# One pool for two attentions, shared places, and q and k split at their projection, in a hybrid decoder layer on one Trainium2 core

## The chip, the cores and the metric

The kernel runs on one core of one Trainium2 chip. The metric is the time of one execution on the device in microseconds (us). Five engines work side by side and meet through semaphores: PE (TensorE, matmuls; PEld is its weight load), DVE (VectorE), ACT (ScalarE), POOL (GpSimd) and SP (SyncE, which only issues transfers here). ACT and POOL issue transfers too. Each engine executes its own instructions in a fixed order.

## The reference, cut to what matters

```python
h = rms_norm(x, norm_mix_g)
proj = h @ w_in                                  # (1024, 1024) @ (1024, 5896)
# dilated attention: 3 groups (window, step) = (128,1), (512,4), (2048,16), 4 heads of 64 each
o_g, lse_g = dilated_window_attention(q_g, k_g, v_g, window, step, slopes)
o_a = sum(softmax(lse over groups) * o_g)        # (1024, 256)
# forgetting attention ("fox"), 8 heads of 64, causal, decay = cumsum(log_sigmoid(f))
o_b = softmax(q k^T / 8 + c_t - c_s) @ v         # (1024, 512)
gates = sigmoid(proj[gate columns] + b_gate)     # (1024, 2048)
x = x + (g_a * (o_a @ w_dil_out) + g_b * (o_b @ w_fox_out)) @ w_out
x = x + (silu(h2 @ w_g) * (h2 @ w_u)) @ w_ffn_down     # h2 = rms_norm(x), width 2816
return rms_norm(x, norm_final_g)
```

Everything is fp32; sequence 1024, width 1024.

## The kernel before, in words

Operands of the large products are kept as two fp32r halves, hi and lo (`split`, L94: ACT writes hi, DVE writes lo = source - hi), and a product is three matmuls, hi·hi, hi·lo and lo·hi (`mm3`, L98). Tiles live in pools; a pool that is opened takes the places of one that was closed, and a tile's first write waits until what stood in its place has been read for the last time. The code is written in one order, and a scheduler then lays down the order of each engine, so that a matmul of a later line can stand between two of an earlier one.

The stages, in the order of time: the norm and the value projections; the sums of the normed input for a seven-product scheme; six calls of `projections` (L279), four for the q and k of fox, two for four q and k tiles of the dilated attention; fox (`fox_qk`, `fox_scores`, `fox_values`); the dilated attention (`dil_qk`, `dil_scores`, `dil_values`); the merge with the gates; the output product; the feed-forward part.

**A call of projections** (L279) makes two 128-column blocks. It loads two raw weight tiles (`raw_w`, tag "wr", two places), and `left_side` (L252) makes four operands of them: A1 (split of the first raw tile), S12 and S34 (sums on POOL, L264, L265, L268, L269, then split) and A22 (split of half the second raw tile, two places). Seven groups of twelve matmuls (`prod`, L272) follow. In the order on PE a call overlaps the next: S12 of call n+1 stands ahead of A22 of call n. At the end the two result tiles "qo" are joined on DVE and stored by POOL (L314).

**Fox** takes four pairs of heads. For each, `fox_qk` loads q and k in eight transfers of 64 rows through SP (L558), ACT casts (L559) and DVE takes the remainders (L563, L566). `fox_scores` makes the scores of 512 queries (b = 0 or 1) of one head with two matmuls per key block (L583, L584), ACT adds the decay (L587), POOL masks (L590), DVE takes the maxima and POOL reduces them over partitions (L598). `fox_values` subtracts and sums on DVE (L611, L614, L623), exponentiates on ACT (L617) and multiplies with the values (L634) and with ones (L637); `finish` (L323) divides. Values of one unit are written behind the scores of the next one.

**The dilated attention** does the like in four units (u, b): scores L342, evicted on DVE (L700, L710, L720), maxima and sums in `over_keys` (L734), POOL's reduction L726, subtraction L747 to L755, exponentials on ACT, values L780 and ones L783. Its pools "dil" and "dila" open after fox's "fox" and "foxa" have been closed; its q and k come by `dil_qk` (L677, ACT's queue), its values by `load_vd` (L665, POOL's queue).

**Fill.** `ahead` (L214) is a plain projection of one block, 48 matmuls with 512 columns (L99 to L101, tile "pf"): 8 blocks of q and k of the dilated attention (`BESIDE`) and 16 blocks of gates. The scheduler puts these 1152 matmuls between those of the attentions, where PE would wait. ACT evicts each half (L224) into one tile "fst" of 4 KB per partition and stores it with one transfer (L225). The last gate may only start behind the last values of the dilated attention (L807).

Behind the attentions the pool "gates" opens; its first tile "oh" lies on the places of "fst". `load_o` (L819) brings the attentions' results and splits them, and the merge's matmuls (L189, L190, L193) begin.

Of the kernel before, what the change touches and what calls it, by code (L numbers as in the profile page):

```python
# [8 lines left out]
F32 = mybir.dt.float32  # L9
F32R = mybir.dt.float32r  # L10
# [5 lines left out]
P = 128  # L16
# [31 lines left out]
def layer_kernel(  # L48
# [34 lines left out]
    o_dram = dpool.tile([6, P, S], F32, name="o_dram")  # L83

# [119 lines left out]
    fqk_dram = dpool.tile([2, 4, P, S], F32, name="fqk_dram")  # L204
# [9 lines left out]
    def ahead(pool, c0, dst, dl=1, sc=1.0):  # L214

        pf = [psf.tile([P, HALF], F32, tag="f", name=nm("pf")) for _ in range(2)]
        w = load_w(w_in[:, c0:c0 + P], KT, P)
        for hh in range(2):
            for k in range(KT):
                mm3(pf[hh][:], w[:, k], hT[hh][:, k], k == 0, k == KT - 1)  # L220
        n = HALF // dl
        st = pool.tile([P, dl, S // dl], F32, tag="fst", name=nm("fst"), bufs=2)
        for hh in range(2):
            nc.scalar.activation(out=st[:, :, hh * n:(hh + 1) * n], in_=view(pf[hh][:], dl), func=AF.Copy, scale=sc)  # L224
        nc.scalar.dma_start(out=dst, in_=st[:].rearrange("p r i -> p (r i)"))  # L225
# [26 lines left out]
    def left_side(pool, rg, ru, bufs):  # L252
# [9 lines left out]
        S34, A22, A1 = pair(KT, "s34", 1), pair(4, "a22", 2), pair_of(rg[:])  # L262
# [16 lines left out]
    def projections(pool, T, c, dst, dls, sc):  # L279
# [33 lines left out]
        for o, d in zip((o2, o1), dst[::-1]):  # L313
            nc.gpsimd.dma_start(out=d, in_=o[:].rearrange("p r i -> p (r i)"))  # L314
# [93 lines left out]
    with pool_of("comb1", 1) as tpool:  # L408
# [90 lines left out]
        with pool_of("proj", 1) as upool:  # L499
            cums = [upool.tile([P] + d, F32, name=n, bufs=1) for n, d in (  # L500
                ("sums", [2, P]), ("az", [NT * 8]), ("u", [NT * 8]), ("t1", [NT * 8]), ("tot", [NT, 8]))]
            for pr in range(0, 4, 2):
                for a in range(2):
                    c0 = FOX0 + a * FOX_W + pr * P
                    projections(upool, T, (c0, c0 + P), [fqk_dram[a, pr + i] for i in range(2)], (1, 1), 1.0)
# [40 lines left out]
    with pool_of("fox", 1) as spool:  # L546
        vf = spool.tile([P, NT, 4, 2, DH], F32, name="vf", bufs=1)
        nc.gpsimd.dma_start(out=vf[:].rearrange("p t a b d -> p t (a b d)"), in_=vf_dram.rearrange("t p c -> p t c"))

        def fox_qk(pool, ql, pr):  # L550
# [3 lines left out]
            for a, xs, sc in ((0, qx, SCALE), (1, kx, 1.0)):  # L554
                for e in range(2):
                    raw = pool.tile([P, S], F32, tag="qraw", name=nm("qraw"), bufs=2)
                    for at in half:
                        nc.sync.dma_start(out=raw[at, :], in_=fqk_dram[a, pr, half[e], :])  # L558
                    nc.scalar.activation(out=xs[e][:], in_=raw[:], func=AF.Copy, scale=sc)  # L559
                    rows = half[e] if a == 0 else half[1 - e]  # L560
                    hi = xs[e][rows, :].bitcast(F32)
                    if a == 0:
                        nc.vector.scalar_tensor_tensor(out=ql[e][rows, :], in0=raw[rows, :], scalar=sc, in1=hi,  # L563
                                                       op0=ALU.mult, op1=ALU.subtract)
                    else:
                        nc.vector.tensor_tensor(out=xs[e][rows, :], in0=raw[rows, :], in1=hi, op=ALU.subtract)  # L566
# [75 lines left out]
        with pool_of("foxa", 2) as apool:  # L642
            pend = None
            ql = [apool.tile([P, S], F32R, name=f"ql{e}", bufs=1) for e in range(2)]
            for e in range(2):
                nc.gpsimd.memset(ql[e][half[1 - e], :].bitcast(F32), 0.0)
            for pr in range(4):
                qk = fox_qk(apool, ql, pr)
                for b in range(2):
                    unit = [fox_scores(apool, qk, 2 * pr + e, b) for e in range(2)], pr, b  # L650
                    if pend:
                        fox_values(apool, *pend)
                    pend = unit
            fox_values(apool, *pend)

    for u, g, a in BESIDE:
        ahead(fpool, dil_cols(u, g, a), dqk_dram[u, g, a], STR[a][g], (SCALE, 1.0)[a])


    with pool_of("dil", 1) as spool:  # L660
        vd, last_pv = [None, None, None], [None]

        def load_vd(pool, g):
            vd[g] = pool.tile([P, NT, 2, 2, DH], F32, tag=f"vd{g}", name=nm("vd"), bufs=1)
            nc.gpsimd.dma_start(out=vd[g][:].rearrange("p t a b d -> p t (a b d)"),  # L665
                                in_=vd_dram[g].rearrange("t p c -> p t c"))

        load_vd(spool, 0)
        load_vd(spool, 1)

        def dil_qk(pool, u):

            qk = [[None, None] for _ in range(3)]
            for g in range(3):
                for a in range(2):
                    qk[g][a] = pool.tile([P, STR[a][g], S // STR[a][g]], F32, tag=f"qk{g}{a}", name=nm("dqk"), bufs=1)
# [3 lines left out]
        def dil_scores(pool, qk, u, b):  # L680
# [3 lines left out]
            L0, L2, Mx, L1 = [[pool.tile([P] + d, F32, tag=n, name=nm(n), bufs=bufs) for e in range(2)]  # L684
                              for n, d, bufs in (("L0", [NT, P], 3), ("L2", [4, P], 3),
                                                 ("Mx", [HALF], 4), ("L1", [2, 2, 256], 3))]
# [72 lines left out]
        def dil_values(pool, scs, u, b, o):  # L759
# [24 lines left out]
            finish(pool, po, den, o[:, b::2])  # L784
            if b == 1:
                nc.gpsimd.dma_start(out=o_dram[u], in_=o[:])

        with pool_of("dila", 1) as apool:
            pend = None
            for u in range(2):  # L790
                qk = dil_qk(apool, u)
                for b in range(2):
                    scs = dil_scores(apool, qk, u, b)
                    if b == 0:
# [291 lines left out]
```

## Time and profile before

| what | value |
|---|---|
| median of 3 runs | 1523.96 us (1522.74 to 1524.77) |
| the profiled execution's own time | 1522.51 us |
| its span, first to last instruction | 1520.2 us |
| granted TensorE clock, mean | 0.992 |
| first fox score (L583) on PE | 290.16 us from the start |
| first dilated score (L342) | about 521 us |
| last dilated values and ones (L780, L783) | end at about 651.7 us |
| first matmul of the merge (L189) | 668.21 us |

A row of the page or of a list of groups has line, engine, operation, output<-inputs, shapes and count; behind the first bar the busy time in us and the mean of one in ns, behind the second bar the idle time of the engine just before, and what ended it. A row of the timeline begins with start and duration in us; in brackets stands the idle time before it and who ended it. A row of the windows has the stretch, its length, then for each engine the busy time and the number of instructions, the granted TensorE clock, the share of the transfer engines and GB/s.

### The profile page before, as it was taken

The numbers are of one execution on the slowest core, as the hardware profiler recorded it, in microseconds if no ns is written. First come the engines' busy times: TensorE is split into PE (matmuls) and PEld (weight loads), VectorE is DVE, ScalarE is ACT, GpSimd is POOL, SyncE is SP. The second block draws the span as 40 slices with busy tenths as digits, with TensorE's granted clock in tenths as the row PEclk, the third lists the DMA queues.
The fourth block names the chain that finished last, engine by engine and source line by source line (L and its number), as shares of the span: only waits on it lengthen the run. The fifth ranks groups of instructions, "written<-read, shape, count | busy, mean of one in ns | idle before, by whom it ended". The sixth has DMA issues, their size and how long they took to land.

```text
span 1520.2 us, 18124 instructions
## 1 busy us (share of the span) xinstructions
PE 1472.8 (97%) x6956; PEld 1192.0 (78%) x6956; DVE 894.1 (59%) x1321; ACT 536.8 (35%) x808; POOL 418.4 (28%) x351
## 2 busy tenths in 40 slices
PE   7999999999999999789999999999999999999997
PEld 6899888867777777568888788888888877888886
DVE  6482433398898399936628854444444445856546
ACT  5232221476566132335315432222222225312113
POOL 1012321273353011100000155555555553140000
PEclk9999999999999999989999999999999999999999
DMA  8132334733332732155613122222222225642202
GB/s 257 42 98 63 111 97 121 226 113 102 110 99 69 257 122 66 56 181 180 242 56 139 42 69 84 83 83 83 84 83 83 84 97 197 204 139 84 96 15 97
DMA packets 139045, 171.60 MB, mean 113 GB/s; under 512 B 6992, under 2 KB 108368, under 8 KB 138960
## 3 DMA queue, kind: packets, MB, share of 16 engines
q1 hardware_dynamic: 118096, 105.95, 23.5%
q0 software_dynamic: 9616, 34.62, 6.1%
q10 hardware_dynamic: 11248, 29.89, 5.3%
q8 instruction: 54, 0.88, 0.2%
q14 instruction: 31, 0.25, 0.1%
HBM read 123.25 MB, written 47.19 MB: 112 GB/s over the span
## 4 chain that ended last, share of the span: by engine, by line
PE 85%; DMA 4%; DVE 3%; ACT 3%; POOL 3%; issue 2%; SPq 0%; ACTq 0%; POOLq 0%; DVEq 0%
PE pd L276 26%; PE pd L99 10%; PE pd L100 10%; PE pd L101 10%; PE pf L100 5%; PE pf L101 5%; PE pf L99 5%; DMA wr<-in_w_ffn_in_dram 2%; PE pd L189 2%; PE pd L634 2%; PE pd L190 2%; PE pd L193 2%; ACT wh L95 2%; POOL sg L994 1%; PE pd L780 1%
## 5 line engine op out<-in xcount | busy, mean ns | idle before, releaser
L96 DVE TENSOR_TENSOR wl<-wr,wh 128x1024 fp32r<-128x1024 f32 (+2 forms) x152 | 165.9, 1095 | 147.3 <-ACT wh L95 146.7
L95 ACT ACTIVATE wh<-wr 128x1024 fp32r<-128x1024 f32 (+2 forms) x152 | 140.6, 932 | 316.2 <-PE pd L100 91.9
L276 PE MATMUL pd<-hT_t,wh 128*128 128x512 f32 x784 | 242.2, 390 | 1.4 <-ACT cc L289 0.7
L276 PE MATMUL pd<-tT,wh 128*128 128x512 f32 x672 | 206.9, 389 | 0.4 <-DVE v L909 0.4
L276 PEld LDWEIGHTS pd<-hT_t,wh 128*128 128x128 f32 x784 | 147.0, 188 | 32.4 <-ACT c L977 1.1
L276 PE MATMUL pd<-hT_t,wl 128*128 128x512 f32 x392 | 153.9, 393 | 1.7 <-DVE wl L96 1.5
L99 PE MATMUL pf<-hT_t,wh 128*128 128x512 f32 x384 | 151.0, 393 | 0.6 <-ACT fst L224 0.6
L100 PE MATMUL pf<-hT_t,wh 128*128 128x512 f32 x384 | 151.0, 393 | 0.0
L101 PE MATMUL pf<-hT_t,wl 128*128 128x512 f32 x384 | 150.9, 394 | 0.0
L276 PEld LDWEIGHTS pd<-tT,wh 128*128 128x128 f32 x672 | 126.1, 188 | 27.0 <-DVE v L909 0.8
L99 PE MATMUL pd<-wh,wh 128*128 128x512 f32 x352 | 137.6, 392 | 3.4 <-DVE acc L1037 1.9
L100 PE MATMUL pd<-wl,wh 128*128 128x512 f32 x352 | 137.1, 389 | 0.0
L101 PE MATMUL pd<-wh,wl 128*128 128x512 f32 x352 | 137.0, 389 | 0.0
L276 PE MATMUL pd<-tT,wl 128*128 128x512 f32 x336 | 130.1, 390 | 0.0
L1037 DVE TENSOR_TENSOR acc<-pd,acc 128x512 f32<-128x512 f32 x128 | 85.6, 685 | 69.2 <-PE pd L101 69.1
L264 POOL TENSOR_TENSOR s<-wr 128x512 f32<-128x512 f32 x26 | 38.9, 1496 | 312.8 <-DVE tT L96 196.0
L96 DVE TENSOR_TENSOR wl<-s,wh 128x1024 fp32r<-128x1024 f32 x52 | 64.7, 1246 | 66.6 <-ACT wh L95 63.7
L95 ACT ACTIVATE wh<-s 128x1024 fp32r<-128x1024 f32 x52 | 55.1, 1060 | 126.5 <-POOL s L265 95.1
L276 PEld LDWEIGHTS pd<-hT_t,wl 128*128 128x128 f32 x392 | 73.6, 188 | 22.2 <-DVE wl L96 7.3
L101 PEld LDWEIGHTS pf<-hT_t,wl 128*128 128x128 f32 x384 | 72.1, 188 | 19.8 <-issue 5.0
L99 PEld LDWEIGHTS pf<-hT_t,wh 128*128 128x128 f32 x384 | 72.1, 188 | 19.7 <-issue 4.6
L100 PEld LDWEIGHTS pf<-hT_t,wh 128*128 128x128 f32 x384 | 72.1, 188 | 18.5 <-issue 4.1
(228 smaller groups left out, 2776.8 us busy)
## 6 DMA issues: line engine op xcount, KB each, us to landing
wr<-in_w_in_dram SPq DMA_DIRECT2D x46, 512.0 KB, 4.3
wr<-in_w_ffn_in_dram SPq DMA_DIRECT2D x44, 512.0 KB, 4.3
wr<-a_dram SPq DMA_DIRECT2D x22, 512.0 KB, 4.3
wr<-in_w_ffn_down_dram SPq DMA_DIRECT2D x22, 512.0 KB, 3.7
a_dram<-a POOLq DMA_DIRECT2D x20, 512.0 KB, 5.0
qraw<-fqk_dram SPq DMA_DIRECT2D x32, 256.0 KB, 4.2
g_dram<-fst ACTq DMA_DIRECT2D x16, 512.0 KB, 2.9
land<-g_dram SPq DMA_DIRECT2D x16, 512.0 KB, 3.4
```

Source lines behind the costliest of these rows:

```text
L95: nc.scalar.activation(out=hi, in_=src, func=AF.Copy)
L96: return nc.vector.tensor_tensor(out=lo, in0=src, in1=hi.bitcast(F32), op=ALU.subtract)
L99: nc.tensor.matmul(psum, w.hi, m.hi, start=start, stop=False)
L100: nc.tensor.matmul(psum, w.hi, m.lo, start=False, stop=False)
L101: last_mm[0] = nc.tensor.matmul(psum, w.lo, m.hi, start=False, stop=stop)
L189: nc.tensor.matmul(pt[hh][:], w.hi[:, k], m.hi, start=(k == 0), stop=False)
L190: nc.tensor.matmul(pt[hh][:], w.hi[:, k], m.lo, start=False, stop=False)
L193: nc.tensor.matmul(pt[hh][:], w.lo[:, k], m.hi, start=False, stop=(k == kt - 1))
L264: nc.gpsimd.tensor_tensor(out=s12[:, :4], in0=u1, in1=u2, op=ALU.add)
L276: last_mm[0] = nc.tensor.matmul(bank[:], p, q, start=first and k == 0 and n == 0, stop=k == 3 and n == 2, skip_group_check=True)
L634: nc.tensor.matmul(po[half[e], HALF - width[j]:], vf[:, j, pr, e], L[:, off[j]:off[j + 1]], start=(j == nj - 1), stop=(j == 0), skip_group ...
L1037: nc.vector.tensor_tensor(out=acc[:, t, cs], in0=pt[:], in1=acc[:, t, cs], op=ALU.add)
```

## The change

- One pool "attention" holds the tiles of both attentions. Those of the second that take over places of the first carry the same tag: its q and k those of fox's kx, qx and ql, its values the place of vf, its L0 tiles those of fox's score tiles of b = 0; the places of fox's score tiles of b = 1 (`over`) hold its third value tile and half of its L0 and L1.
- The last `fox_values` is written behind the first `dil_scores`, so that scores of the second attention stand among the last values of the first.
- `projections` of fox's q and k splits its results (ACT into "qh", one place, DVE in place) and stores hi and lo; POOL issues four transfers per call in place of two. The scale is applied there. `fox_qk` only loads, ten transfers of 64 rows per pair, on ACT's queue; ACT's casts and DVE's remainders there go.
- A22 has one place in `projections` (it had two).
- `ahead` evicts and stores each half by itself, into tiles of half the size; for blocks with a step the store has pieces of 512/step elements.
- The dilated result is kept by halves of the queries and put in order when it is split for the merge.

```diff
-    fqk_dram = dpool.tile([2, 4, P, S], F32, name="fqk_dram")
+    fqk_dram = dpool.tile([2, 4, 2, P, S], F32, name="fqk_dram")
...
-        st = pool.tile([P, dl, S // dl], F32, tag="fst", name=nm("fst"), bufs=2)
         for hh in range(2):
-            nc.scalar.activation(out=st[:, :, hh * n:(hh + 1) * n], in_=view(pf[hh][:], dl), func=AF.Copy, scale=sc)
-        nc.scalar.dma_start(out=dst, in_=st[:].rearrange("p r i -> p (r i)"))
+            st = pool.tile([P, dl, n], F32, tag="fst", name=nm("fst"), bufs=2)
+            nc.scalar.activation(out=st[:], in_=view(pf[hh][:], dl), func=AF.Copy, scale=sc)
+            nc.scalar.dma_start(out=dst.rearrange("p (r i) -> p r i", r=dl)[:, :, hh * n:(hh + 1) * n], in_=st[:])
...
-        S34, A22, A1 = pair(KT, "s34", 1), pair(4, "a22", 2), pair_of(rg[:])
+        S34, A22, A1 = pair(KT, "s34", 1), pair(4, "a22", bufs), pair_of(rg[:])
...
         for o, d in zip((o2, o1), dst[::-1]):
-            nc.gpsimd.dma_start(out=d, in_=o[:].rearrange("p r i -> p (r i)"))
+            flat = o[:].rearrange("p r i -> p (r i)")
+            if hl:
+                hi = pool.tile([P, S], F32R, tag="qh", name=nm("qh"), bufs=1)
+                split(hi[:], flat, flat)
+                nc.gpsimd.dma_start(out=d[0], in_=hi[:].bitcast(F32))
+                nc.gpsimd.dma_start(out=d[1], in_=flat)
...
+            for e in range(2):
+                q, k = [fqk_dram[a, pr, :, half[e], :] for a in range(2)]
+                for to, src in ((kx, k), (qx, (q[0], q[0]))):
+                    for i in range(2):
+                        nc.scalar.dma_start(out=to[e][half[i], :].bitcast(F32), in_=src[i])
+                nc.scalar.dma_start(out=ql[e][:DH, :].bitcast(F32), in_=q[1])
...
-            fox_values(apool, *pend)
...
+        for u in range(2):
+            qk = dil_qk(apool, u)
+            for b in range(2):
+                scs = dil_scores(apool, qk, u, b)
+                if u == b == 0:
+                    fox_values(apool, *pend)
+                    pend = None
+                    vd01 = apool.tile([P, 2, NT, 2, 2, DH], F32, tag="v", name="vd01", bufs=1)
+                    ov1, ov2 = over(), over()
...
+                if pend:
+                    dil_values(apool, *pend)
+                pend = scs, u, b
+        dil_values(apool, *pend)
```

How the order moves. In the rows below, numbers behind an L are lines of the file in question; the changed file's `split` is L96 and L97.

First, ACT in the middle of the projections, before: wh<-wr with 512 columns is A22, wh<-s is S34 and then S12, cc and qo evict PE's first bank.

```order
L289 ACTIVATE cc_1467<-pd_1496 128x512
L95 ACTIVATE wh_1474<-s_200_1489 128x1024
L289 ACTIVATE qo_1465<-pd_1496 128x512
L95 ACTIVATE wh_1732<-wr_1724 128x1024
L95 ACTIVATE wh_1739<-s_237_1736 128x1024
L95 ACTIVATE wh_1730<-wr_1726 128x512
L289 ACTIVATE cc_1594<-pd_1623 128x512
```

The same stretch in the changed kernel:

```order
L291 ACTIVATE cc_1483<-pd_1512 128x512
L96 ACTIVATE wh_1490<-s_204_1505 128x1024
L96 ACTIVATE qh_1451<-qo_1321 128x1024
L96 ACTIVATE wh_1636<-s_223_1633 128x1024
L291 ACTIVATE qo_1481<-pd_1512 128x512
L96 ACTIVATE wh_1764<-wr_1756 128x1024
L96 ACTIVATE wh_1627<-wr_1623 128x512
L96 ACTIVATE qh_1606<-qo_1482 128x1024
L291 ACTIVATE cc_1618<-pd_1647 128x512
```

Two splits of results (qh) have come in per call. The A22 that stands here is that of the next call in the changed kernel, where it was that of the call after the next; the load of the raw tile behind it moves with it. On POOL, per call, the order was L264, L265, two stores, L268, L269; it is now the sums of L264, L268 and L265, two stores, that of L269, two stores.

Second, DVE where the attentions meet, in the changed kernel: Mx_3104 is the sum of exponentials of fox's last head (`fox_exp`), Mx_3718 and Mx_3719 are the maxima of the first dilated unit.

```order
L628 TENSOR_TENSOR Mx_3104<-Mx_3104,L_3103 128x512
L738 TENSOR_TENSOR Mx_3719<-Mx_3719,L_510_3701 128x4x128
L738 TENSOR_TENSOR Mx_3718<-Mx_3718,L_509_3700 128x4x128
L628 TENSOR_TENSOR Mx_3104<-Mx_3104,L_3103 128x512
L718 SCALAR_TENSOR_TENSOR L_514_3705<-R_2011,pd_3767 128x512
L718 SCALAR_TENSOR_TENSOR L_513_3704<-R_2011,pd_3766 128x512
L628 TENSOR_TENSOR Mx_3104<-Mx_3104,L_3103 128x512
L740 TENSOR_TENSOR Mx_3719<-Mx_3719,L_514_3705 128x2x256
```

Before, all of fox's sums (L623) and its last division (L333) stand ahead of the first dilated eviction (L700). On PE, 73 matmuls of fill, fox's last values (16 matmuls L634), 1 of fill, the ones (L637) and 74 of fill stood there in a row ahead of the first dilated score; now 32 dilated scores and 47 of fill stand ahead of those values, and 22 of fill between them and the ones.

Third, ACT at the end of the attentions, before: the last exponential (L756), the last division (L327, L328), the eviction of the last gate's halves (L224), its store, and the first split of the merge.

```order
L756 ACTIVATE L_598_4172<-L_598_4172 128x1024
L327 ACTIVATE rc_4375<-pd_4339 128x512
L328 ACTIVATE rc_4375<-rc_4375 128x512
L224 ACTIVATE fst_5340<-pf_5284 128x512
L95 ACTIVATE wh_5418<-wr_5420 128x512
L224 ACTIVATE fst_5340<-pf_5285 128x512
L225 DMA g_dram<-fst_5340 128x1024
L95 ACTIVATE oh_5348<-land_5350 128x1024
```

The changed kernel from its last exponential on:

```order
L754 ACTIVATE over_3855<-over_3855 128x1024
L96 ACTIVATE wh_5052<-wr_5054 128x1024
L226 ACTIVATE fst_4985<-pf_4927 128x512
L227 DMA g_dram<-fst_4985 128x512
L336 ACTIVATE rc_4360<-pd_4323 128x512
L337 ACTIVATE rc_4360<-rc_4360 128x512
L226 ACTIVATE fst_5044<-pf_4988 128x512
L227 DMA g_dram<-fst_5044 128x512
L96 ACTIVATE wh_5114<-wr_5116 128x1024
L226 ACTIVATE fst_5047<-pf_4989 128x512
```

Ten more evictions of gate halves follow there, with their stores, ahead of the first split into oh. On PE, 48 matmuls of fill stood behind the last ones (L783) before, and 276 stand there now. Between the last three dilated scores and the last values stood 23 of fill, the values and ones of the unit before, and 17 of fill, with nothing behind them; now the values and ones of the unit before, 52 of fill, one matmul of the last values, 23 of fill, and the other 31. The fill ahead of the first fox score is 160 matmuls before and 134 now.

## What the change does to the time: the prediction

> **What bounds the kernel now.** I read the head of the page first: PE is busy for 1472.8 of 1520.2 us, so little but PE's own idle time can be won.
>
> ```profile
> span 1520.2 us, 18124 instructions
> PE 1472.8 (97%) x6956; PEld 1192.0 (78%) x6956; DVE 894.1 (59%) x1321; ACT 536.8 (35%) x808; POOL 418.4 (28%) x351
> ```
>
> The groups by line say where PE stood and whom it waited for. In the stages that the change touches two groups carry nearly all of it: the dilated values (L780), which waited 8.8 us for ACT's exponential, and the merge's first matmul (L189), which waited 5.4 us for the split into oh.
>
> ```profile
> L780 PE MATMUL pd<-L,vd 128*64 128x128 f32 (+2 forms) x256 | 20.5, 324 | 8.8 <-ACT L L756 8.8
> L189 PE MATMUL pd<-oh,wh 128*128 128x512 f32 x96 | 36.9, 401 | 5.4 <-ACT oh L95 5.4
> ```
>
> The windows (length, then PE, PEld, DVE, ACT, POOL, the clock, the transfer share) show what comes with such a wait: the granted clock falls to 0.50 and stays there after work resumes. They also show the stretches that I need below.
>
> ```profile
> 160.00:240.00 80.00, 80.00 (x354) 66.24 (x354) 31.67 (x41) 20.05 (x24) 23.86 (x23) 1.00 0.35 112
> 290.00:651.00 361.00, 347.15 (x1888) 256.79 (x1888) 292.81 (x490) 175.29 (x302) 109.49 (x100) 0.99 0.35 109
> 500.00:520.00 20.00, 20.00 (x89) 14.46 (x86) 3.30 (x4) 3.97 (x6) 3.28 (x4) 1.00 0.79 281
> 540.00:600.00 60.00, 60.00 (x378) 44.66 (x377) 57.48 (x94) 23.06 (x33) 7.84 (x5) 1.00 0.28 97
> 636.00:640.00 4.00, 0.00 (x0) 0.00 (x0) 3.93 (x7) 0.56 (x2) 1.78 (x1) 0.86 0.69 197
> 644.00:648.00 4.00, 4.00 (x26) 2.52 (x24) 1.93 (x3) 0.00 (x0) 0.00 (x0) 0.50 0.00 0
> 668.00:672.00 4.00, 3.79 (x9) 3.02 (x10) 3.81 (x4) 3.00 (x4) 0.55 (x2) 0.50 0.33 125
> ```
>
> From 290 us (first fox score) to 651 us (last ones) PE idles 361 - 347.15 = 13.85 us, of which 8.78 are the one wait at the end. There the fill has run out, and the last unit's chain on DVE and ACT lies bare. Why it comes so late stands at 500 to 520: while the pools change, DVE works 3.30 of 20 us and PE lives on fill alone. A matmul of 512 columns takes 80.00 / 354 = 0.226 us.
>
> **The end of the attentions.** The chain of waits (start, duration, what) and the timeline price the two waits.
>
> ```profile
> 625.16 4.39 PE pd L780 x64
> ```
>
> ```profile
> 643.66 7.15 PE L780 MATMUL pd<-L,vd 128*64 128x256 f32 x64 [8.78 <-ACT L L756]
> ```
>
> The same 64 instructions took 4.39 us at full clock and 7.15 behind the wait: it costs 8.78 + 2.76 us. In the changed order the values and ones of the unit before and 52 of fill stand between the last scores and these values: 4.4 + 0.9 + 11.8 = 17.1 us, and 23 more of fill (5.2 us) between the first and the second of them. What the chain needs there, by the rows from 635 to 643 us, of which these are the kinds that count:
>
> ```profile
> 636.02 0.69 DVE L742 TENSOR_TENSOR Mx<-Mx,L 128x512 f32<-128x512 f32 x1
> 636.87 1.78 POOL L726 PARTITION_ALL_REDUCE Mx<-Mx  x1 [13.02 <-DVE Mx L742]
> 637.34 1.12 DVE L331 SCALAR_TENSOR_TENSOR den<-den,rc 128x512 f32<-128x512 f32 x1
> 642.55 1.06 ACT L756 ACTIVATE L<-L 128x1024 f32<-128x1024 f32 x1 [0.57 <-DVE L L755]
> ```
>
> Two evictions and seven additions or maxima of 0.7 us, the reduction of 1.8, 3.7 of subtractions (five of 0.7 or a little more) and 1.1 of exponential make 13 us for the first head; the division (0.7, 1.1 and 0.7) and the second head's subtractions make it 19 for the second. Against that stand 17 and 22. So both go: **-8.78 and -2.76**. The fill for this is there: 276 matmuls now stand behind the last ones, where 48 stood, 62 us of pure matmuls instead of 11.
>
> What is late next is the merge, as before: oh lies on the places of fst, and waits for the last store.
>
> ```profile
> 663.73 0.33 ACTq L225 DMA_DIRECT2D g_dram<-fst  x1
> 667.11 3.90 ACT L95 ACTIVATE oh<-land 128x1024 fp32r<-128x1024 f32 x4 [3.40 <-DMA g_dram<-fst]
> 668.21 2.08 PE L189 MATMUL pd<-oh,wh 128*128 128x512 f32 x4 [5.44 <-ACT oh L95]
> 673.30 1.09 PE L189 MATMUL pd<-oh,wh 128*128 128x512 f32 x4
> ```
>
> That last store is now half as large. Issue to landing was 3.3 us here; other stores show this:
>
> ```profile
> g_dram<-fst ACTq DMA_DIRECT2D x16, 512.0 KB, 2.9
> dqk<-dqk_dram ACTq DMA_DIRECT2D x12, 512.0 KB, 6.6
> vd_dram<-vst ACTq DMA_DIRECT2D x8, 256.0 KB, 2.1
> out_dram<-xf ACTq DMA_DIRECT2D x8, 256.0 KB, 2.5
> ```
>
> So 2.1 to 2.5, and **-1.0**. The twelve matmuls from 668.21 to 673.30 took 5.1 us for 2.7 of work, 2.4 lost to the clock. With 4.4 us of idling left I can't tell if the clock drops again: 5.44 did it, and the 1.45 us at 538 us did not. I take half, **-1.2** (0 to -2.4). [...]
>
> **The projections.** The added splits cost 8 × 1.06 us on ACT and 8 × 1.23 on DVE, which in 160 to 240 us are busy for 25% and 40% and gate nothing by that alone. The second split of a call waits until the first store has left qh (3 us); ACT has nothing due before S12 some 4 us later. What isn't covered is A22 with one place, because the raw tile of the call after next is loaded into the place that its split leaves, and POOL's sums and S12 wait for that load. The rows of such a turn:
>
> ```profile
> 183.14 0.63 ACT L95 ACTIVATE wh<-wr 128x512 fp32r<-128x512 f32 x1 [1.60 <-PE pd L276]
> 183.98 0.68 DVE L96 TENSOR_TENSOR wl<-wr,wh 128x512 fp32r<-128x512 f32 x1
> 188.79 1.29 POOL L268 TENSOR_TENSOR s<-wr,wr 128x512 f32<-128x512 f32 x1 [0.95 <-DVE wl L96]
> 185.86 1.06 ACT L95 ACTIVATE wh<-s 128x1024 fp32r<-128x1024 f32 x1 [1.17 <-PE pd L276]
> DMA to landing us min/median/max: 3.7/4.0/5.5
> ```
>
> The last row is of the raw tiles' loads (L243) in this stage. From the end of A22's matmuls: splits 1.5, load 3.7 to 5.5, three sums 4.0 with their gaps, split 1.1, hand-overs 0.2: 10.5 to 12.3 us. PE has 48 matmuls, 10.9 us, until it wants S12. So 0 to 1.4 us are bare, with the lower half of S12 0 to 1.7, in each of four calls; the stores of hi and lo run beside the load, so I don't take the lower end: 0.75 each, **+3.0** (0 to +6.8). Before, this load had a whole call more.
>
> **Inside the attentions.** What leaves and what comes:
>
> ```profile
> L559 ACT ACTIVATE kx<-qraw 128x1024 fp32r<-128x1024 f32 x8 | 8.5, 1061 | 13.3 <-DMA qraw<-fqk_dram 13.3
> L563 DVE SCALAR_TENSOR_TENSOR ql<-qraw,qx 64x1024 fp32r<-64x1024 f32 x8 | 10.5, 1313 | 0.9 <-ACT qx L559 0.8
> L566 DVE TENSOR_TENSOR kx<-qraw,kx 64x1024 fp32r<-64x1024 f32 x8 | 9.7, 1218 | 6.6 <-ACT kx L559 6.5
> qraw<-fqk_dram SPq DMA_DIRECT2D x32, 256.0 KB, 4.2
> vd<-vd_dram POOLq DMA_DIRECT2D x3, 1024.0 KB, 9.3
> ```
>
> ACT loses 16 casts of 1.06 us and gets 64 more issues of 0.33 (40 loads, 24 stores), 17 against 21 us at 49% of the stretch busy; DVE loses 20.2. PE sees neither directly. The loads are new on the path: each head's five wait for that head's last score and stand in ACT's queue ahead of evictions of scores. Until the head's next score PE has, where it is tightest, 16 score matmuls, 23 of fill, 8 of values and 2 ones, about 11 us; five issues (1.7) and a landing of 4.2 fit, and so would one of 8. The three value tiles are loaded behind the first unit's reduction, some 5 us after fox's last values; with 9.3 us and the issues they land after some 17, and PE has 66 of fill, 32 scores and the ones, over 20. So no wait is planned bare, but the stretch is denser: PE's part shrinks to 347.15 - 2.8 - 228 × 0.226 = 292.9 us, and DVE keeps 292.81 - 20.2 - 5.5 (five gates' splits at 1.1) = 267, 91% where it was 81%. From 540 to 600 us it ran at 96% and PE never stood. I add **+1.5** for waits of the kind that make up the other 5.07 us now (-5.07 if all go, +6 if they double).
>
> **The sum.** -8.78 - 2.76 - 1.0 - 1.2 + 3.0 + 1.5 = -9.24 us, on the profiled execution's 1522.51: 1513.3. That execution lies 1.45 us under the median of the three runs, so the median should come to 1514.7.
>
> **Rivals.** First, the loads of fox's q and k are not covered: the row of dqk's loads, six at a time, shows 6.6 us where the raw tiles of L243, of the same size, show 4.0. With 6.6, the five issues (1.7) and four instructions of 1.06 us ahead of them in ACT's queue a head's five take 12.5 us, so 1.5 of them are bare at six head changes, +9: 1523.7, no change. Against it: ACT issues the first ones while that head's last blocks are still being evicted.
>
> Second, it gets slower: the chain on DVE, at 91%, falls behind the order, which spends 228 matmuls less of fill ahead of the last values, so that PE waits for evictions and sums at every unit between 300 us and the end. It decides from 9.24 + 3.05 = 12.3 us on, 4.2% of 292.9; at 7% it is 20.5 us, and with the 1.5 taken out 1533.7. For it speaks 96% from 540 to 600 as a full engine; against it, that PE stood nowhere in those 60 us.
>
> Third, the small pieces: five blocks have step 8, so ten stores have pieces of 64 elements, 256 bytes, where a row of 4 KB was written. If such a store lands later than two halves of fill take (10.9 us), fst isn't free, ACT stops at the eviction and fill stops with it. The slowest store of the trace's fst landed after 12.7 us:
>
> ```profile
> DMA to landing us min/median/max: 2.6/2.9/12.7
> ```
>
> At that, 1.8 us are bare ten times, +18: 1532.7. Nothing here has such pieces from ACT; vd_dram's stores in pieces of 1 KB landed after 2.1 us. [...]
>
> Fourth, it doesn't do what it says: the last unit's wait stays, because the fill ahead of it is spent sooner than planned. Then -1.0 - 1.2 + 4.5 = +2.3: 1526.3.
>
> **How the numbers follow.** A measurement of this kernel can tell about 0.2%, 3.05 us, from no change: faster is under 1520.9, slower over 1527.0. Chances: forecast 0.72, uncovered loads 0.08, DVE 0.08, small pieces 0.05, wait stays 0.07. The forecast's own ends: -8.78 - 2.76 - 1.2 - 2.4 - 5.07 = -20.2, 1503.8; and 1514.7 + 3.8 + 4.5 = 1523.0. With the first rival the range is 1504 to 1524, with 0.8. Faster is the forecast and the better part of the first rival (0.03): 0.75; the same is the rest of it and the fourth: 0.12; slower the second and third: 0.13.
>
> **What would show it.** Right: L780 without a wait over 2 us and at full clock, over 60 us of pure fill behind the last ones, L189's wait near 4.4 us, PE waits of 0.5 to 1.5 us at S12 of the later calls. Wrong: waits of L583 for transfers at head changes (first rival), of L342, L637 or L780 for DVE all along (second), of ACT at fst's evictions for stores (third), or over 4 us of idling at a call's S12 (the projection term).

## The result, and the profile after

The changed kernel takes 1531.20 us (median; 1530.85 to 1534.89), the kernel before 1523.83 us on the same chip: ratio 1.0055, 95% interval 1.0039 to 1.0071. It is slower by about 8 us, where 9 us less had been forecast. The profiled execution is 9.3 us longer than that of before. First the head of its page:

```profile
span 1529.5 us, 18174 instructions
PE 1477.5 (97%) x6956; PEld 1194.4 (78%) x6956; DVE 888.2 (58%) x1313; ACT 527.9 (35%) x800; POOL 410.9 (27%) x361
```

DVE, ACT and POOL do a little less than before, as the change means them to. PE works 4.7 us longer on the same 6956 matmuls, and idles 52.0 us where it idled 47.4. Most of the longer work is lost clock: in windows of 1 us, busy time multiplied by what the granted clock lacks of 1 adds up to 10.9 us, 6.8 before.

The last values (L778 here) have no wait over 0.2 us, and run at full clock (mean 1.00 from 591.2 to 679.8 us). The merge's first matmul (L190) waits a little less than before:

```profile
609.41 1.63 PE L778 MATMUL pd<-over,vd 128*64 128x128 f32 x26
...
679.37 1.65 PE L190 MATMUL pd<-oh,wh 128*128 128x512 f32 x4 [4.42 <-ACT oh L96]
```

The new time stands at two other places. The first is ahead of fox. The groups by line show a wait of fill for ACT's eviction, 0.6 us before (first row, L99 there) and 5.8 us now (second row). The windows show PE idle from 282.9 to 288.7 us, the transfer engines full (a share of 1.08 in the measure of the windows), and the clock down behind it, to 0.50 from 287.36 us on, for 6.83 us:

```profile
L99 PE MATMUL pf<-hT_t,wh 128*128 128x512 f32 x384 | 151.0, 393 | 0.6 <-ACT fst L224 0.6
L100 PE MATMUL pf<-hT_t,wh 128*128 128x512 f32 x384 | 153.1, 399 | 5.8 <-ACT fst L226 5.8
```

```profile
282.00:290.00 8.00, 2.20 (x7) 1.51 (x7) 0.40 (x1) 1.97 (x3) 0.00 (x0) 0.83 1.08 265
```

ACT's timeline there shows what it did meanwhile. ACTq rows are issues; a row with x2 spans both, with what stands between them:

```profile
273.39 0.53 ACTq L227 DMA_DIRECT2D dqk_dram<-fst  x1
273.95 2.14 ACTq L570 DMA_DIRECT2D kx<-fqk_dram  x2
276.12 3.31 ACTq L570 DMA_DIRECT2D qx<-fqk_dram  x2
279.47 0.61 ACTq L571 DMA_DIRECT2D ql<-fqk_dram  x1
280.12 5.63 ACTq L570 DMA_DIRECT2D kx<-fqk_dram  x2
285.79 1.26 ACTq L570 DMA_DIRECT2D qx<-fqk_dram  x2
287.53 0.45 ACTq L571 DMA_DIRECT2D ql<-fqk_dram  x1
288.03 0.60 ACT L226 ACTIVATE fst<-pf 128x512 f32<-128x512 f32 x1 [14.67 <-DMA kx<-fqk_dram]
```

For 14 us ACT issues the first pair's ten loads, and the eviction that frees fill's bank stands behind them. The second kx of the row at 280.12 begins at 285.30 us. The store of 273.39 landed at 285.28, 11.89 us later; the view of the tile fst, in the window of that one store, has

```profile
DMA to landing us min/median/max: 11.9/11.9/11.9
```

That load doesn't read fst. But in this trace every transfer has a semaphore: the 332 of SP and ACT carry eight, one after the other, in one turn for both queues, and none of the 324 that have an earlier one with their semaphore was issued before that had landed. In the changed kernel eight issues, seven of them ACT's, follow such a landing within 0.15 us; in the kernel before it is none of 292. The issue at 285.30 waits, by the trace, for its own semaphore (number 113), the one that the store of 273.39 carries; it begins 0.02 us behind that store's landing. The ten issues themselves add up to 8.7 of ACT's 14 us. But the last one, at 287.53, stood behind a landing at 287.51, so slow issues alone don't explain when the eviction began.

The second place is the dilated part. PE's waits from 470 to 615 us (in all, how many, the longest):

```profile
PE pd L781 <- DVE Mx L740: 4.0, 3, 1.6
PE pd L351 <- DVE den L339: 2.2, 1, 2.2
PE pd L351 <- DVE o L342: 0.9, 1, 0.9
PE pd L351 <- DVE L L708: 0.6, 1, 0.6
```

All are for DVE, and twice the clock halves behind them:

```profile
480.00:600.00 120.00, 111.80 (x715) 80.37 (x714) 115.40 (x190) 39.84 (x61) 21.50 (x16) 0.96 0.33 110
533.00:537.00 4.00, 4.00 (x22) 2.90 (x22) 4.00 (x9) 2.36 (x4) 0.00 (x0) 0.57 0.00 0
584.00:592.00 8.00, 7.16 (x16) 4.50 (x17) 6.96 (x11) 1.23 (x2) 3.83 (x2) 0.57 0.01 2
```

DVE is busy for 115.4 of the 120 us, PE idles 8.2, and 0.43 × (4.00 + 7.16) = 4.8 us more are lost to the clock. Meanwhile 276 matmuls of fill lie unused until the last ones are done.

### The profile page after: what moved, and what is told of

It is laid out like the page before. It is cut to its first block, busy times and chain, and to the rows that moved or that the text cites. A ratio compares the mean times of both kernels' runs of the same rounds, so it can differ in the third digit from the quotient of the medians.

```text
span 1529.5 us, 18174 instructions
## 1 busy us (share of the span) xinstructions
PE 1477.5 (97%) x6956; PEld 1194.4 (78%) x6956; DVE 888.2 (58%) x1313; ACT 527.9 (35%) x800; POOL 410.9 (27%) x361
## 4 chain that ended last, share of the span: by engine, by line
PE 77%; DVE 8%; DMA 6%; ACT 4%; POOL 3%; issue 2%; ACTq 0%; SPq 0%; DVEq 0%; POOLq 0%
PE pd L278 23%; PE pd L100 10%; PE pd L102 10%; PE pd L101 10%; PE pf L100 5%; PE pf L101 4%; PE pf L102 4%; DMA wr<-in_w_ffn_in_dram 3%; ACT wh L96 2%; PE pd L190 2%; PE pd L191 2%; PE pd L194 2%; DVE wl L97 2%; POOL sg L1009 1%; PE pd L639 1%
## 5 line engine op out<-in xcount | busy, mean ns | idle before, releaser
L97 DVE TENSOR_TENSOR wl<-wr,wh 128x1024 fp32r<-128x1024 f32 (+2 forms) x152 | 165.4, 1091 | 189.3 <-ACT wh L96 185.6
L96 ACT ACTIVATE wh<-wr 128x1024 fp32r<-128x1024 f32 (+2 forms) x152 | 140.8, 932 | 360.7 <-PE pd L101 89.3
L100 PE MATMUL pf<-hT_t,wh 128*128 128x512 f32 x384 | 153.1, 399 | 5.8 <-ACT fst L226 5.8
L101 PE MATMUL pf<-hT_t,wh 128*128 128x512 f32 x384 | 152.9, 398 | 0.0
L97 DVE TENSOR_TENSOR wl<-s,wh 128x1024 fp32r<-128x1024 f32 x52 | 67.0, 1289 | 63.8 <-ACT wh L96 60.8
L96 ACT ACTIVATE wh<-s 128x1024 fp32r<-128x1024 f32 x52 | 55.0, 1060 | 117.5 <-POOL s L267 93.7
```

What stands on the lines that cost most here:

```text
L96: nc.scalar.activation(out=hi, in_=src, func=AF.Copy)
L97: return nc.vector.tensor_tensor(out=lo, in0=src, in1=hi.bitcast(F32), op=ALU.subtract)
L100: nc.tensor.matmul(psum, w.hi, m.hi, start=start, stop=False)
L101: nc.tensor.matmul(psum, w.hi, m.lo, start=False, stop=False)
```

## The experiments

Ratios are against the kernel before, run on the same chip. Where nothing else is said, an experiment is the changed kernel with the edit shown.

**The loads on SP.**

```diff
-                        nc.scalar.dma_start(out=to[e][half[i], :].bitcast(F32), in_=src[i])
-                nc.scalar.dma_start(out=ql[e][:DH, :].bitcast(F32), in_=q[1])
+                        nc.sync.dma_start(out=to[e][half[i], :].bitcast(F32), in_=src[i])
+                nc.sync.dma_start(out=ql[e][:DH, :].bitcast(F32), in_=q[1])
```

> The changed kernel with one edit: fox_qk's ten loads per pair are issued on SP's queue, not ACT's. Theory one (ACT's queue): ACT sat from 273.95 to 288.03 us in the issue of the first pair's ten loads, because a load may only be issued when the transfer eight before it has landed, and the evictions of fill stood behind them. On SP nothing of PE's stands behind them, so PE's wait of 5.8 us at 282.9 us goes, and the 2.75 us of halved clock behind it: 1531.2 - 8.5 = 1522.7 us, ACT's eviction of fst on time. Rival (the bytes): the loads land at 291 to 296 us whoever issues them, and the fill's raw weights wait behind them on SP, so PE waits as long at the next fill block or at the first score: 1529 to 1532 us.

1517.02 us, ratio 0.9966 (0.9954 to 0.9978): faster than before. PE has no wait over 0.2 us from 250 us to the dilated part:

```profile
280.00:290.00 10.00, 10.00 (x47) 8.32 (x47) 1.23 (x1) 1.66 (x2) 0.00 (x0) 1.00 1.10 280
```

The transfer engines are as full as in the changed kernel (1.10 in that row, 1.08 there), and the loads land late as well (the first head's five by 288.4 us, the second's by 293.8, and each of the second head's issues stood behind the landing eight places earlier). But now SP waits for that, and ACT evicts. Theory one held, the rival fell. The gain is larger than expected, 0.9% or 13.6 us for 8.5: the dilated part's waits came out smaller too, 4.2 us for 8.2, in an order that the scheduler laid down anew (from 300 us on, PE's order differs).

**Half of the loads on SP**: those of each pair's second head.

> The changed kernel with the five loads of each pair's second head on SP's queue and the five of the first head on ACT's. Theory one (ACT is held because a transfer of ACT or SP may only start when the one eight before it, of either queue, has landed): with five loads, a store and a raw tile ACT meets no such landing; it is busy with five issues for 5 to 6 us, PE's wait of 5.8 us at 283 us is under 1.5 and the clock holds, so the time is that of all loads on SP, 0.996 to 0.998 of the kernel before. Rival (each issue on ACT is slow because the transfer engines are full, and that alone holds the evictions): half the issues, half the wait: 2.5 to 3 us and some halved clock stay, 0.999 to 1.002.

1526.39 us, ratio 1.0024 (1.0016 to 1.0033). Neither number came: PE waits 6.2 us. ACT's timeline, and the landing of the raw tile of fill that SP issued at 272.10:

```profile
271.90 2.14 ACTq L570 DMA_DIRECT2D kx<-fqk_dram  x2
274.07 9.96 ACTq L570 DMA_DIRECT2D qx<-fqk_dram  x2
285.89 0.45 ACTq L571 DMA_DIRECT2D ql<-fqk_dram  x1
```

```profile
DMA to landing us min/median/max: 11.5/11.5/11.5
```

The second qx begins at 283.58 us, when that raw tile has landed (283.56). My count was wrong, not the mechanism: SP's five loads take places in the same turn of eight, so ACT meets a landing at its fourth load.

**Stores in one piece.**

```diff
-            nc.scalar.dma_start(out=dst.rearrange("p (r i) -> p r i", r=dl)[:, :, hh * n:(hh + 1) * n], in_=st[:])
+            nc.scalar.dma_start(out=dst[:, hh * HALF:(hh + 1) * HALF], in_=st[:].rearrange("p r i -> p (r i)"))
```

> The changed kernel with the halves of the fill stored in one piece of 2 KB per partition, where the blocks with step 4 or 8 had pieces of 256 or 512 bytes. The columns of these blocks of the dilated q and k then stand in another order, so the second and third group work on permuted columns; the amount of work is the same. Rival (small pieces): the store of the second half landed after 11.89 us because it has 1024 pieces of 256 bytes, and ACT waited for just that landing; in one piece it lands after some 5 us, PE's wait of 5.8 us at 283 us shrinks to under 1, and the kernel takes 1522 to 1525 us. Theory one (the ten loads and the 2 MB of vf fill the transfer engines by themselves): the small pieces are 0.5 of some 6 MB, the landing comes 1 to 2 us sooner, and the wait falls by as much: 1528 to 1531 us.

This kernel leaves the columns out of the order that the second and third group need, so it doesn't compute the layer; the amount of work is the same. 1533.72 us, ratio 1.0074 (1.0061 to 1.0086). Neither number came. The store now lands after 6.5 us, for 11.9 in the changed kernel, about as the rival had it, and PE's wait grows all the same, to 13.8 us. ACT stops one load later, for the raw tile that SP issued at 272.37 and that landed after 20.0 us, at 292.40:

```profile
271.59 0.34 ACTq L227 DMA_DIRECT2D dqk_dram<-fst  x1
...
275.44 3.09 ACTq L570 DMA_DIRECT2D kx<-fqk_dram  x2
292.42 1.10 ACTq L570 DMA_DIRECT2D qx<-fqk_dram  x2
```

So the small pieces made that store slow, but it was only the first landing to stop ACT; without it the next one does.

**Six loads for ten.**

```diff
+                nc.scalar.dma_start(out=kx[e][:].bitcast(F32), in_=fqk_dram[1, pr, :, half[e], :])
+                nc.scalar.dma_start(out=qx[e][:].bitcast(F32), in_=q[0].unsqueeze(0).broadcast_to([2, DH, S]))
                 nc.scalar.dma_start(out=ql[e][:DH, :].bitcast(F32), in_=q[1])
```

> The changed kernel with the ten loads per pair, of 64 rows each, joined to six on the same ACT queue: k hi and lo in one of 128 rows, q hi twice in one of 128 rows from a repeated source, q lo. The bytes are the same. Theory one (each load takes one of eight places among the transfers of ACT and SP, and the ninth waits for the first to land): six loads, a store and a raw tile just fit, ACT is held for under 3 us instead of 14, and most of the 8.5 us go: 1522 to 1526 us. Rival (the bytes and the slow issue on a full queue): the issue lasts as long per byte, so the wait stays: 1529 to 1532 us.

1643.27 us, ratio 1.0793 (1.0779 to 1.0807). Neither number came, and this says nothing on the theories, since the joined loads themselves are slow: 60 GB/s were moved from 290 to 300 us (row in the last section), where it was 280 from 280 to 290 with the loads on SP.

**The split alone**, with the loads on SP or on ACT. Both are the kernel before, with its two pools and whole stores, q and k split in projections, A22 in one place, and fox_qk of the changed kernel.

> The kernel before with one part of the change alone: fox's q and k are split where they are made (with A22 in one place, which that needs), and loaded as hi and lo on SP; the two pools, the order of the two attentions and the fill's whole stores stay. Theory three (what ends the last unit's wait is that the dilated part starts earlier, which the shared places and the lighter DVE each give a part of): 76 matmuls of fill stand behind the last ones where 48 stood, 6.3 us, so some 2.5 of the 8.8 us of wait stay; against it A22's 3.5: 0.996 to 0.999 of the kernel before. Rival (the lighter DVE and ACT do all of it, the shared pool nothing): as all of the change with loads on SP, 0.9966 or less, and no wait at the last values. Second rival (the pools' change holds the dilated part up as before): the whole wait stays, 1.001 to 1.003.

> The kernel before with the split of q and k where they are made (A22 in one place), in two pools as before, and the ten loads per pair on ACT's queue, as the change has them. Theory one (ACT held at the head of fox by landings): against the same kernel with the loads on SP, 0.9924, a wait of 5 to 8 us comes at fill near 282 us with some halved clock: 8 to 11 us, 0.998 to 1.000 of the kernel before. Rival (the wait needs the half stores of the change, which here are whole): 0.992 to 0.994.

On SP 1510.61 us, 0.9924 (0.9911 to 0.9938); on ACT 1529.22 us, 1.0049 (1.0035 to 1.0063). The queue alone costs 1.25%, 19 us; 8 to 11 had been expected. On ACT, PE's wait at fill is

```profile
PE pf L99 <- ACT fst L224: 14.0, 1, 14.0
```

and ACT's timeline has the same picture, for a raw tile that SP issued at 273.47 and that landed after 19.7 us:

```profile
276.25 4.83 ACTq L565 DMA_DIRECT2D kx<-fqk_dram  x2
293.24 1.10 ACTq L565 DMA_DIRECT2D qx<-fqk_dram  x2
```

The stores are whole here, so the wait doesn't need halves. On SP the last unit's wait of 8.8 us is gone with only 76 matmuls of fill behind the last ones, and between 495 and 640 us a single wait for DVE is left:

```profile
PE pd L349 <- DVE L L700: 1.4, 1, 1.4
```

Theory three fell, its rival held: the split, with the lighter DVE and ACT that it brings, does it, and the shared pool isn't needed for it. A22 in one place, which comes with it, doesn't: with that alone (below) the wait is still 7.0 us.

**No overlap of the attentions**, loads on SP: the last fox_values is written ahead of the first dil_scores.

> The changed kernel with all loads of fox's q and k on SP, and the last fox_values written ahead of the first dil_scores, so that the two attentions no longer overlap in the written order (56 matmuls of fill more stand ahead of the first dilated score; 252 still stand behind the last ones). Theory two (PE's waits between 505 and 600 us come from DVE, which has the sums of fox's last unit and the evictions and maxima of the first dilated units at once): they shrink from 4.2 us and 3 us of halved clock to under 2 in all, and nothing is lost at the end, since fill covers it: 0.992 to 0.996 of the kernel before. Rival (DVE's work is the bound wherever it stands, the order of it doesn't matter): the same waits come some 15 us later: 0.996 to 0.998.

1521.89 us, ratio 1.0000 (0.9991 to 1.0008): 0.34% slower than with the overlap. Theory two as I had put it fell, and the rival's number didn't come either. The waits are there without the overlap, and larger:

```profile
PE pd L781 <- DVE Mx L740: 5.8, 2, 3.5
PE pd L351 <- DVE over L698: 1.8, 1, 1.8
```

Here 252 matmuls stand behind the last ones; with two pools and the same lighter DVE (the split alone) it was 76 and next to no wait. That led to the theory as mended: not the overlap, but how little fill stands between the dilated units (from the first dilated score to the last ones 257 matmuls here, 369 in the split alone).

**Gates between the units**, loads on SP. The fill is the same, only written elsewhere:

```diff
+        def gates(a, z):
+            for br, dt in merge_order[a:z]:
+                ahead(fpool, GATE0 + (br * KT + dt) * P, g_dram[br * KT + dt])
...
         for u in range(2):
             qk = dil_qk(apool, u)
             for b in range(2):
+                gates(done, (6, 8, 10, 12)[2 * u + b])
+                done = (6, 8, 10, 12)[2 * u + b]
                 scs = dil_scores(apool, qk, u, b)
```

> The changed kernel with all loads of fox's q and k on SP, and the fill placed otherwise: six, eight, ten and twelve of the gates' blocks are written ahead of the first, second, third and fourth unit of dilated scores, where all sixteen were written behind the units. Ahead of the last dilated score stand 969 matmuls of fill instead of 790, behind the last ones 120 (27 us) instead of 296. Theory two, mended (DVE is the bound where both attentions run; the shared pool lets the dilated units come closer together and leaves the fill behind them, where nothing needs cover; the 296 are missing where PE waits): the waits for DVE between 475 and 640 us fall from 4.2 us to under 1.5 and no clock is lost there, 0.9966 - (2.7 + 3.05)/1522 = 0.993 of the kernel before. Rival (DVE works the same span of time and PE waits for it wherever the fill stands): 0.996 to 0.998.

1506.97 us, ratio 0.9906 (0.9890 to 0.9921), the fastest kernel here; 0.993 had been expected. PE has no wait for DVE left between 460 and 625 us. The dilated part's waits and clock, 4.2 and 3.05 us with the loads on SP alone, account for 7.2 of the 9.0 us between the two profiled executions. The windows over the dilated part, with the loads on SP alone, and then with the gates between:

```profile
470.00:590.00 120.00, 115.84 (x749) 82.24 (x748) 115.02 (x191) 38.56 (x60) 22.70 (x15) 0.97 0.32 107
```

```profile
480.00:620.00 140.00, 140.00 (x928) 104.42 (x928) 116.81 (x188) 43.43 (x64) 20.16 (x15) 1.00 0.34 112
```

DVE does the same 115 to 117 us of work. In 120 us it is full and PE waits; in 140 us, with 179 more matmuls on PE, it isn't, and the 20 us are not lost, since that fill had to be done anyway.

**A22 in one place alone**, in the kernel before.

> The kernel before with one edit: A22 has one place in projections, where it had two. Theory (the chain from A22's release over the raw tile's load, POOL's sums and S12's split): PE waits of 1.1 to 1.2 us at S12 in three or four of the later calls, 3.5 us, and where the granted clock falls after one of them 1.6 more, as in the changed kernel: 1527 to 1529 us. Rival (the waits come from the added splits of qo and POOL's added stores): nothing changes, 1523 to 1525 us.

1525.96 us, ratio 1.0024 (1.0015 to 1.0033), 3.7 us. The size came near what was expected, but not as four waits: in the projections PE's idle time grows by 2.3 us, from 0.7 to 3.0, half of it one wait of 1.1 us and the rest waits of 0.2 us or less. The other 1.4 us aren't traced to A22.

**A22 in two places**, loads on SP, with room made by splitting q and k by halves and by putting the decay's tiles into a place of the results.

> The changed kernel with all loads on SP, and A22 with two places as in the kernel before; the room comes from splitting q and k by halves of 512 columns through a tile of half the size, and from tiles of the decay that stand in a place of the results. Theory (A22's one place costs what the kernel before lost with it alone, 0.24%): 0.9966 - 0.0024 = 0.994 of the kernel before. Rival (the added splits and POOL's added stores are what PE waits for at S12): no gain, 0.996 to 0.998.

1537.66 us, ratio 1.0102 (1.0086 to 1.0119). A miss: the room costs more than the place. PE waits at the decay, where tiles of the decay and results now share places:

```profile
PE pd L497 <- DVE lf L493: 8.2, 1, 8.2
PE pd L278 <- DVE qo L296: 4.9, 1, 4.9
```

That the sharing makes these waits is read from the edit, not tried. The run tells nothing on A22 in the changed kernel.

**Gates' halves in the split alone**: fill's gates evicted and stored by halves, through four tiles of 2 KB.

> The kernel before with the split alone and the loads on SP, as measured at 0.9924, and the gates' blocks of fill evicted and stored by halves of 512 columns through four tiles of 2 KB (blocks with a step stay whole). Theory (the last store is half as large, so the merge's wait for oh falls from 5.4 to 4.4 us): 0.9924 - 0.0007 = 0.9917 of the kernel before, or 0.990 if the clock now holds behind it. Rival (the same as in the pooled kernel, 4.4 us still halve the clock, and added stores cost ACT): 0.992 to 0.9935.

1513.02 us, ratio 0.9946 (0.9933 to 0.9958), against 0.9924 with whole stores. Neither number came: the merge's wait falls from 5.4 to 4.4 us, and the kernel is slower. The two traces differ by 2.0 us in the clock lost, 4.8 for 2.8: it halves behind a wait of 1.45 us at 516 us and one of 2.2 at 1281, where it held behind waits of 1.45 and 1.3 in the split alone.

## Why the prediction was wrong

**The end of the attentions**: right. The last values' wait of 8.78 us and the 2.76 of halved clock behind it are gone, as forecast. The reason given, that fill and the overlap cover the chain, is more than was needed: the split alone removes the wait too.

**The last store**: right. 5.44 fell to 4.42, where -1.0 had been forecast. The clock still halves behind it; the loss in 1 us windows is 1.7 us where it was 2.4, so -0.7 for -1.2.

**The projections**: the term was mis-sized on the low side. PE's idle time there goes from 0.7 to 4.7 us, and the clock falls once for 1.6 us more; together +5.6, forecast +3.0 (0 to +6.8). A22 by itself brings 2.3 us of idling. The other 1.7 us and the clock I had not seen; the last section shows them. That the sum stays inside the range is luck.

**The loads on ACT**: this step failed. I wrote: "five issues (1.7) and a landing of 4.2 fit, and so would one of 8", and of ACT's 64 added issues of 0.33 against the casts that go: "PE sees neither directly". Both look at one head in the middle of fox. The first pair has ten loads at once, beside the 2 MB of vf, a store and a raw tile; an issue takes 0.45 to 2.0 us there, a landing 8 to 13, and the load that stands eight places behind the store of 273.39 was issued at 285.30, when that had landed (285.28). So it wasn't PE that waited for a load, as my first rival had it (L588 waits 0.8 us in all for one), but ACT, with fill's eviction queued behind it: 5.8 us and 2.75 of clock, forecast 0. Measured by moving the queue, it is worth 13.6 us in the changed kernel, part of it in the dilated part, and 19 in the split alone. The trace of before had a hint of it: the first four of the same loads, on SP, took 0.51 to 1.01 us each to issue, and 4.8 to 7.9 us to land. I took the issue from a row of one store.

```profile
L558 SPq DMA_DIRECT2D qraw<-fqk_dram x4: 512/587/1014, 262.2 to 264.1; - x4
DMA to landing us min/median/max: 4.8/5.7/7.9
```

**Inside the attentions**: this term was too small, +1.5 for measured +8.9 (idle time 5.1 to 9.2 us from 290 to 600, and 4.8 of clock where none was lost). It is the second rival at a smaller size: DVE at 96% in the dilated part. The step that failed is the argument against it, "PE stood nowhere in those 60 us": there PE had 293 matmuls of fill around the dilated units in 131 us, now 286 in 136 us together with the last values and sums of fox. I counted the 276 matmuls behind the last ones as cover, and did not ask where they were missing; the 16.5 us from the last ones to the merge before would hold some 73 (an estimate, at 0.226 us each). In the kernel with the loads on SP, where 296 stood there, the waits are gone once 176 of them are moved back between the units.

**The sum** of the measured terms is -11.5 - 1.0 - 0.7 + 5.6 + 8.6 + 8.9 = +9.9 us, beside +9.3 in the spans; small differences in later stages make up the rest. The third rival had a part too: the small pieces made one store land after 11.9 us, 6.5 in one piece. But in one piece the kernel was no faster.

What stays open: why DVE falls behind what the scheduler laid down, by a few per cent in its durations or by its order, was not tried by itself.

## What to carry to other kernels

An issue on an engine that also computes can be a wait in that engine's queue, and where many transfers start together its price can be a landing: here ten issues held ACT for 14 us, where 0.33 each had been reckoned, and a landing took 11.89. So price issues by the rows of the busiest place, and follow each to the instructions queued behind it. Fill behind the last wait is worth only what that wait needs; the rest belongs where an engine close to 100% (DVE at 96% here) would make PE wait. And test a change's parts alone: here one part was worth -0.76%, and the queue on which it was done +1.25%.

## What the runs showed of the hardware that I had not expected

**Joined loads at 60 GB/s.** While the joined loads of 128 rows were under way, from 290 to 300 us, the transfers moved 60 GB/s, at a busy share of 0.16 of the 16 engines:

```profile
290.00:300.00 10.00, 0.00 (x0) 0.00 (x0) 0.00 (x0) 0.00 (x0) 0.00 (x0) 0.50 0.16 60
```

In the kernel with ten loads of 64 rows on SP they moved 280 GB/s at a share of 1.10, from 280 to 290 us. The source of the joined loads has an outer dimension of two; whether that is why they are slow was not shown, since no run here changes that dimension alone. The issues behind these loads are held as well: four of the six took 5.8 to 10.5 us.

**DVE and POOL took longer side by side.** In the changed kernel DVE's remainder of qo runs beside one of POOL's sums, and its split of the sums beside the last of them:

```profile
192.71 2.27 POOL L267 TENSOR_TENSOR s<-s,wr 128x512 f32<-128x512 f32 x1
196.04 1.29 POOL L271 TENSOR_TENSOR s<-wr,s 128x512 f32<-128x512 f32 x1
```

```profile
192.18 1.66 DVE L97 TENSOR_TENSOR qo<-qo,qh 128x1024 f32<-128x1024 f32 x1 [2.04 <-ACT qh L96]
196.10 2.33 DVE L97 TENSOR_TENSOR wl<-s,wh 128x1024 fp32r<-128x1024 f32 x1 [2.27 <-ACT wh L96]
```

The first sum and the split in the kernel before with A22 in one place, where DVE has no remainder to make there:

```profile
193.64 1.29 POOL L265 TENSOR_TENSOR s<-s,wr 128x512 f32<-128x512 f32 x1
```

```profile
196.06 1.32 DVE L96 TENSOR_TENSOR wl<-s,wh 128x1024 fp32r<-128x1024 f32 x1 [5.81 <-ACT wh L95]
```

The split that PE waits for there ends at 198.4 us in the one and at 197.4 in the other, and the changed kernel has a wait of 1.17 us at that matmul where the other has 0.17. In both pairs the one that began later took 1.0 us longer than the like one in the other kernel (2.27 for 1.29 us, 2.33 for 1.32), nearly what the earlier one still had to run (1.1 and 1.2 us). Why was not shown.

**The clock fell after a wait of 1.2 us.** In the changed kernel it halved at 198.61 us, for 3.41 us, behind a wait of 1.17 us, well under the 5.44 that the prediction had seen to do it; in the kernel with the loads on SP it did not behind the like wait of 1.18 us at 196.9, nor in the changed kernel itself behind one of 1.18 that ended at 220.94:

```profile
198.00:202.00 4.00, 3.52 (x9) 2.75 (x10) 1.72 (x3) 0.47 (x1) 0.00 (x0) 0.58 0.74 207
```

```profile
197.00:201.00 4.00, 2.93 (x13) 2.44 (x14) 2.31 (x3) 0.00 (x0) 0.00 (x0) 1.00 0.86 262
```

The records of the granted clock in two traces, of before and of the changed kernel, show one difference. In the changed kernel it halves at 198.61, 287.36, 533.12, 584.32, 679.89 and 1526.40 us, in the kernel before at 638.92, 666.23, 843.72 and 1516.14; in each trace these times lie multiples of 3.41 us apart. I cut both traces from 12 us on by that step. Of the steps at full clock with PE busy for less than 45%, all 7 were followed by half clock; of those with 45 to 58%, 2 of 6; of the other 856, none. The changed kernel's step with the wait before 198.61, then the one with the wait before 220.94:

```profile
195.20:198.61 3.41, 1.86 (x8) 0.91 (x7) 2.51 (x2) 1.36 (x2) 2.12 (x3) 1.00 0.74 273
```

```profile
219.09:222.50 3.41, 2.23 (x10) 1.50 (x9) 3.08 (x3) 0.00 (x0) 0.70 (x1) 1.00 0.96 308
```

PE was busy for 55% of the one and 65% of the other. These are counts of two traces; what sets the clock they do not show. The waits of 4.4 and 5.4 us at the merge halved it in both, for a loss of 1.7 and 2.4 us. So of two waits of 1.2 us in one kernel the one cost 1.6 us more and the other nothing, and the sum has to hold both.
